# Two weight quarters per pass over the token blocks in an encoder layer's projection

## The chip, the cores and the metric

The kernel runs on one core of a Trainium2 chip. The metric is the device time of one execution in microseconds. Three runs of the kernel before took 2153.36, 2153.40 and 2154.49 us; the median is 2153.4 us.

## The reference

One layer of a hybrid encoder in float32, applied to 1024 prompt tokens and 256 sample tokens, each with 16 learned meta tokens ahead of them. A normalised input goes through one wide projection; eight heads attend globally (two key/value heads), eight in a neighbourhood window with a position bias; both results are gated by silu and go through the output projection.

```python
u = rms_norm(h, norm_w) @ w_in                     # 2048 -> 6656 columns
qa, ka, va, za, qb, kb, vb, zb = jnp.split(u, split_points(), axis=-1)
qa = apply_axial_rope(rms_norm(qa, q_norm_a), tabs)
ka = apply_axial_rope(rms_norm(ka, k_norm_a), tabs)
ya = global_gqa(qa, ka, va) * jax.nn.silu(za)
yb = neighbourhood_attention(rms_norm(qb, q_norm_b), rms_norm(kb, k_norm_b), vb, rpb) * jax.nn.silu(zb)
return h + jnp.concatenate([ya, yb], axis=-1) @ w_out
```

## The kernel before

The projection's 6656 columns are cut into 52 strips of 128 columns. A strip's weights are 16 tiles of 128 x 128 (the sum over 2048), handled as four quarters of four tiles (`WCH`). Every number is kept as a high and a low part (`wh` and `wl`, `xh` and `xl`), and each tile takes three matmuls: high by high (L227), high by low (L228), low by high (L229).

The tokens are done in two chunks. Chunk one has 512 tokens: the 256 of the sample, 240 of the prompt and the meta tokens. Chunk two has the other 784 tokens of the prompt, in two blocks of 512 and 272 columns (`BL`), each with its own bank of PSUM per strip. Their operands stay on chip as tiles `x` (512 columns) and `xb` (272 columns). The output projection follows.

`strips` (L192) projects one strip, or two or three together, over the four quarters in turn. For a quarter it loads the weights (`wr`, L206), then either casts them to `wh` on ScalarE and subtracts for `wl` on VectorE (`split`, L66 and L67), or, in chunk two, casts `wh` (L211) and loads a `wl` that chunk one stored (L210). `wh` and `wl` have four buffers each (pool `w`), so a quarter's buffers are those of the quarter four before it, and its cast and load wait until PE has read that one for the last time. Then PE goes over the blocks: in chunk two twelve matmuls of 512 columns, then twelve of 272 columns, for each quarter. After every second quarter `run_due` issues attention work that is due there.

Chunk two begins with the strips `KA` and `VA` together, in which every pass has twice the matmuls; the other 50 strips go alone. While the global heads run (`attend`), the scheduler of the framework places their matmuls among those of the projection, by its own estimate of when data is ready; later the windowed heads have fixed places (`local_heads`). The last strip is projected with `self.turn` set, with the blocks in reverse order. Transposes of V on PE are held back until the next strip has done quarter and block `self.tie`. In PE's queue, as in those of ScalarE, VectorE and SyncE, instructions stand in the order that the scheduler wrote.

Of the kernel before, what the change touches and what calls it, by code (L numbers as in the profile page):

```python
# [48 lines left out]
WCH = 4  # L49
# [10 lines left out]
class Kern:  # L60
# [131 lines left out]
    def strips(self, jobs, getx):  # L192


        nc, tc = self.nc, self.tc
        out = [[pool.tile([P, 512], F32, tag=tag, name="pp") for pool, tag in pools] for _, _, pools in jobs]
        for c in range(KT // WCH):
            ws = []
            behind = self.behind.pop(0) if self.behind else None
            for j, (s, _, _) in enumerate(jobs):  # L200
                wp = self.w if j < 2 else self.w1
                with tc.high_priority(offset=self.woff), tc.issue_after(behind) if behind else nullcontext():
                    w = self.raw.tile([P, WCH, P], F32, tag="raw", name="wr")
                    cuts = ((0, 1), (1, WCH)) if self.projected == 3 and c == 0 and not self.second else ((0, WCH),)
                    for i, e in cuts:
                        self.lastw = nc.sync.dma_start(w[:, i:e], self.io["w_in"][s][:, c * WCH + i:c * WCH + e, :]).ins  # L206
                    wh = wp.tile([P, WCH, P], F32R, tag="wh", name="wh")
                    wl = wp.tile([P, WCH, P], F32R, tag="wl", name="wl")
                    if self.second and s not in AGAIN:
                        nc.sync.dma_start(wl[:].bitcast(F32), self.wld[s][:, c * WCH:(c + 1) * WCH, :])  # L210
                        nc.scalar.copy(wh[:], w[:])  # L211
                    else:
                        for i, e in cuts:
                            self.lastsplit = self.split(wh[:, i:e], wl[:, i:e], w[:, i:e])
                            self.lasthi = self.hi
                ws.append((wh, wl))
                if not self.second and s not in AGAIN:
                    nc.sync.dma_start(self.wld[s][:, c * WCH:(c + 1) * WCH, :], wl[:].bitcast(F32))
            nb = len(jobs[0][1])
            for b in range(nb)[::-1] if self.turn else range(nb):  # L220
                for k in range(WCH):
                    kt = c * WCH + k
                    xh, xl = getx(kt)[b]
                    first, last = kt == 0, kt == KT - 1
                    for (wh, wl), ps, (_, blocks, _) in zip(ws, out, jobs):
                        p, n = ps[b], blocks[b][1]
                        nc.tensor.matmul(p[:, :n], wh[:, k, :], xh[:, :n], start=first, stop=False)  # L227
                        nc.tensor.matmul(p[:, :n], wh[:, k, :], xl[:, :n], start=False, stop=False)  # L228
                        self.lastmm = nc.tensor.matmul(p[:, :n], wl[:, k, :], xh[:, :n], start=False, stop=last).ins  # L229
                if self.turned and (c, b) == self.tie:  # L230
                    for i in self.turned:
                        tc.add_manual_dep(i, self.lastmm.name, mybir.DependencyInfo(
                            mybir.DependencyClass.NoSync, mybir.DependencyReason.DATA), reason="turned")
                    self.turned = []
            if c % 2:
                self.run_due()
        return out
# [530 lines left out]
    def chunk2(self):  # L768
# [20 lines left out]
        def k_strip(s, g, wc, rope):  # L789
            k, km = k_first(g)  # L790

            def evac(ps):
                for p, (o, n) in zip(ps, BL):
                    rp = (ct[:, o:o + n], st[:, o:o + n]) if rope else None
                    self.qk_evac(p, o, n, wc, rp, [(0, n, k[:, 0, C1P + o:C1P + o + n], k[:, 1, C1P + o:C1P + o + n])])
                return k, km
            return s, BL, evac

        def v_rows_of(s, g):

            def evac(ps):
                for p, (o, n) in zip(ps, BL):
                    self.rows_out(self.v_rows(p, o, n), n, self.vn[g], C1P + o)
            return s, BL, evac

        def v_tiles(g):

            h, l = (self.v.tile([P, 8, P], F32R, tag=f"v{i}", name="va", align_bytes=ALIGN) for i in range(2))
            nc.sync.dma_start(l[:].bitcast(F32), self.vn[g][:].rearrange("(t p) d -> p t d", p=P))
            nc.scalar.copy(h[:], l[:].bitcast(F32))  # L810
            nc.vector.tensor_tensor(out=l[:], in0=l[:].bitcast(F32), in1=h[:].bitcast(F32), op=ALU.subtract)
            return [(h[:, j, :], l[:, j, :]) for j in range(8)], self.load_vm(g)
# [12 lines left out]
        def q_strip(s, h, wc, rope):  # L825
            q = self.q.tile([P, 2, NP], F32R, tag="q", name="q", align_bytes=ALIGN)
            nc.sync.dma_start(q[:, :, :C1P].bitcast(F32), self.qd[h][:])

            def evac(ps):
                for p, (o, n) in zip(ps, BL):  # L830
                    rp = (ct[:, o:o + n], st[:, o:o + n]) if rope else None
                    self.qk_evac(p, o, n, wc, rp, [(0, n, q[:, 0, C1P + o:C1P + o + n], q[:, 1, C1P + o:C1P + o + n])])
                return q
            return s, BL, evac

        def z_strip(s, h):
            z = self.z.tile([P, NP], F32, tag="z", name="z")
            nc.sync.dma_start(z[:, :C1P], self.zd[h][:, :C1P])

            def evac(ps):  # L840
                for p, (o, n) in zip(ps, BL):
                    self.z_evac(p, o, n, [(0, n, z[:, C1P + o:C1P + o + n])])
                return z
            return s, BL, evac
# [39 lines left out]
        def run(h, q, z, k, v):  # L884
            (k, km), (v, vm) = k, v
            for b in range(4):
                c = slice(QB * b, QB * b + QB)
                keys = [(k[:, 0, o:o + P], k[:, 1, o:o + P]) for o in range(0, NP, P)]
                for _ in self.attend(q[:, :, c], z[:, c], keys, km, v, vm[:], self.yd[0][:, 2 * b:2 * b + 2, h, :]):
                    pass  # L890
# [51 lines left out]
        def fill(n):  # L942
            for _ in range(min(n, len(late))):
                pr(late.pop(0))

        for g in range(2):
            if g == 0:
                k, _ = pr(k_strip(KA, 0, kw, True), v_rows_of(VA, 0))
                self.tie = 0, 1
            else:  # L950
                k, = pr(k_strip(KA + g, g, kw, True))
                pr(v_rows_of(VA + g, g))
            v = v_tiles(g)
            for h in range(4 * g, 4 * g + 4):
                z, = pr(z_strip(ZA + h, h) + (((self.sp, "sp"),) if h == 0 else ()))
                q, = pr(q_strip(QA + h, h, qw, True))
                run(h, q, z, k, v)
                fill(FILL)
# [390 lines left out]
```

## Time and profile before

| what | us |
|---|---|
| median of three runs | 2153.4 |
| the profiled execution | 2154.02 |
| its span, first to last instruction | 2152.2 |
| PE busy | 2146.3 |
| VectorE busy | 1675.4 |
| ScalarE busy | 1204.0 |
| chunk two's projection and attention | about 599 to 1756 |

The profiled execution is the one that all rows come from. A matmul's length in the profile is longer than the distance to the next one's start, since they are pipelined: what a matmul costs the engine is read from the starts in the timeline. Idle time shows as a gap between busy stretches, and the chain of waits tells which engine the end of the program hangs on.

### The profile page before, as it was taken

The page shows a single profiled execution, that of the slowest core. Times are in us where ns is not written, and L with a number is a line of the kernel's source. Part 1 is how long each engine was busy: PE and PEld are TensorE (multiplying, and loading weights), DVE is VectorE, ACT ScalarE, POOL GpSimd, SP SyncE. Part 2 cuts the span into 40 slices and gives each one's busy share as a digit, 9 for nine tenths or more (in the row PEclk, how much of TensorE's full clock was granted, in tenths as well). Part 3 has the DMA queues.
Part 4 walks back from the last instruction along what each step waited for, and adds up shares of the span by engine and source line. Part 5 has one row for each costly group of instructions (what it writes and reads, how often), then busy time and mean ns, then how long its engine had stood idle before and what let it go on. Part 6 is the DMA issues. An engine that isn't in the chain of part 4 may idle for free.

```text
span 2152.2 us, 33487 instructions
## 1 busy us (share of the span) xinstructions
PE 2146.3 (100%) x11473; PEld 1866.0 (87%) x11473; DVE 1675.4 (78%) x3053; ACT 1204.0 (56%) x2459; POOL 530.0 (25%) x250
## 2 busy tenths in 40 slices
PE   9999999999999999999999999999999999999999
PEld 7888888888888899998998898989999888888887
DVE  7688987788874899898799898787787886545763
ACT  7677644554665777777677776444444454232230
POOL 1142422222221223232133413333333311000000
PEclk9999999999999999999999999999999999999999
DMA  8657799988654333334333334654433364762663
GB/s 294 215 186 228 242 295 319 348 280 271 212 190 133 99 100 108 109 108 125 100 105 101 106 119 128 206 162 139 133 123 124 114 214 144 241 235 89 235 226 107
DMA packets 257419, 377.21 MB, mean 175 GB/s; under 512 B 43072, under 2 KB 108768, under 8 KB 257248
## 3 DMA queue, kind: packets, MB, share of 16 engines
q1 hardware_dynamic: 257248, 375.07, 54.2%
q8 instruction: 90, 1.47, 0.3%
q14 instruction: 81, 0.66, 0.1%
HBM read 281.01 MB, written 100.38 MB: 177 GB/s over the span
## 4 chain that ended last, share of the span: by engine, by line
PE 99%; DMA 0%; DVE 0%; SPq 0%; issue 0%; ACT 0%
PE pp L227 22%; PE pp L229 22%; PE pp L228 22%; PE pq L1075 6%; PE pq L1074 6%; PE pq L1073 6%; PE po L422 3%; PE po L522 2%; PE sp L488 2%; PE sp L383 2%; PE sp L384 2%; PE sp L382 1%; PE po L423 1%; PE tp L543 0%; PE sm_ps L316 0%; PE sm_ps L315 0%
## 5 line engine op out<-in xcount | busy, mean ns | idle before, releaser
L227 PE MATMUL pp<-x,wh 128*128 128x512 f32 (+1 forms) x1664 | 654.4, 394 | 0.8 <-ACT wh L66 0.8
L228 PE MATMUL pp<-x,wh 128*128 128x512 f32 (+1 forms) x1664 | 648.3, 390 | 0.0
L229 PE MATMUL pp<-x,wl 128*128 128x512 f32 (+1 forms) x1664 | 648.2, 390 | 0.0
L229 PEld LDWEIGHTS pp<-x,wl 128*128 128x128 f32 x1664 | 312.6, 188 | 63.0 <-DVE wl L67 0.6
L227 PEld LDWEIGHTS pp<-x,wh 128*128 128x128 f32 x1664 | 312.6, 188 | 57.8 <-ACT wh L66 3.1
L228 PEld LDWEIGHTS pp<-x,wh 128*128 128x128 f32 x1664 | 312.9, 188 | 53.6
L262 POOL PARTITION_ALL_REDUCE m<-ms x78 | 237.8, 3049 | 324.5 <-ACT ms L260 251.2
L346 POOL PARTITION_ALL_REDUCE tot<-a x80 | 175.8, 2198 | 476.2 <-DVE a L343 449.2
L67 DVE TENSOR_TENSOR wl<-wr,wh 128x512 fp32r<-128x512 f32 (+2 forms) x287 | 212.6, 742 | 102.4 <-ACT wh L66 77.3
L66 ACT CAST wh<-wr 128x512 fp32r<-128x512 f32 (+2 forms) x287 | 174.0, 611 | 163.9 <-PE pp L228 148.9
L228 PE MATMUL pp<-xb,wh 128*128 128x272 f32 x832 | 240.6, 289 | 0.0
L227 PE MATMUL pp<-xb,wh 128*128 128x272 f32 x832 | 239.7, 288 | 0.0
L229 PE MATMUL pp<-xb,wl 128*128 128x272 f32 x832 | 239.4, 288 | 0.0
L1075 PE MATMUL pq<-wm,yl 128*128 128x512 f32 x560 | 218.5, 390 | 0.1
L1073 PE MATMUL pq<-wm,yh 128*128 128x512 f32 x560 | 218.5, 390 | 0.0
L1074 PE MATMUL pq<-wm,yh 128*128 128x512 f32 x560 | 218.2, 390 | 0.0
L328 POOL PARTITION_ALL_REDUCE ma<-m x80 | 109.1, 1364 | 424.7 <-DVE m L326 424.7
L228 PEld LDWEIGHTS pp<-xb,wh 128*128 128x128 f32 x832 | 156.5, 188 | 8.4
L227 PEld LDWEIGHTS pp<-xb,wh 128*128 128x128 f32 x832 | 156.6, 188 | 8.1
L229 PEld LDWEIGHTS pp<-xb,wl 128*128 128x128 f32 x832 | 157.5, 189 | 0.9
L1075 PEld LDWEIGHTS pq<-wm,yl 128*128 128x128 f32 x560 | 105.1, 188 | 22.3 <-DVE yl L67 0.5
L1073 PEld LDWEIGHTS pq<-wm,yh 128*128 128x128 f32 x560 | 105.2, 188 | 21.7
(217 smaller groups left out, 3879.3 us busy)
## 6 DMA issues: line engine op xcount, KB each, us to landing
wr<-in_w_in SPq DMA_DIRECT2D x413, 256.0 KB, 3.4
wld<-wl SPq DMA_DIRECT2D x132, 256.0 KB, 4.2
wl<-wld SPq DMA_DIRECT2D x132, 256.0 KB, 3.1
yr<-yd SPq DMA_DIRECT2D x35, 512.0 KB, 5.2
wq<-in_w_out SPq DMA_DIRECT2D x64, 256.0 KB, 5.1
td<-wq SPq DMA_DIRECT2D x64, 256.0 KB, 4.3
ww<-td SPq DMA_DIRECT2D x64, 256.0 KB, 5.4
ww<-in_w_out SPq DMA_DIRECT2D x48, 256.0 KB, 5.1
```

The lines of the kernel that those rows point to most:

```text
L66: self.hi = nc.scalar.copy(hi, full).ins
L67: return nc.vector.tensor_tensor(out=lo, in0=full, in1=hi.bitcast(F32), op=ALU.subtract).ins
L227: nc.tensor.matmul(p[:, :n], wh[:, k, :], xh[:, :n], start=first, stop=False)
L228: nc.tensor.matmul(p[:, :n], wh[:, k, :], xl[:, :n], start=False, stop=False)
L229: self.lastmm = nc.tensor.matmul(p[:, :n], wl[:, k, :], xh[:, :n], start=False, stop=last).ins
L262: nc.gpsimd.partition_all_reduce(m2[:], ms[:], P, RED.add)
L328: nc.gpsimd.partition_all_reduce(ma[:], m1[:], P, RED.max)
L346: nc.gpsimd.partition_all_reduce(tot[:], a1[:], P, RED.add)
L422: nc.tensor.matmul(po[:], vh, hl[:, i], start=j == 0, stop=False)
L1073: nc.tensor.matmul(ps, yh, wh, start=k == 0, stop=False)
L1074: nc.tensor.matmul(ps, yh, wl, start=False, stop=False)
L1075: self.lastmm = nc.tensor.matmul(ps, yl, wh, start=False, stop=k == 7).ins
```

## The change

In chunk two, for a strip that is projected alone, `strips` now collects two quarters in a list `held` before PE goes over the blocks: 24 matmuls of 512 columns over both quarters, then 24 of 272. A strip has two such rounds where it had four. Chunk one has a single block and is left as it is (`nb > 1`), as are the two strips projected together (`len(jobs) == 1`) and the last strip (`self.turn`). The tie of the V transposes is set to the first pair's block 0, which stands where quarter 0 and block 1 stood.

```diff
--- before.py
+++ after.py
@@ -194,6 +194,7 @@
 
         nc, tc = self.nc, self.tc
         out = [[pool.tile([P, 512], F32, tag=tag, name="pp") for pool, tag in pools] for _, _, pools in jobs]
+        held = []
         for c in range(KT // WCH):
             ws = []
             behind = self.behind.pop(0) if self.behind else None
@@ -217,9 +218,12 @@
                 if not self.second and s not in AGAIN:
                     nc.sync.dma_start(self.wld[s][:, c * WCH:(c + 1) * WCH, :], wl[:].bitcast(F32))
             nb = len(jobs[0][1])
+            held.append((c, ws))
+            if nb > 1 and len(jobs) == 1 and c % 2 == 0 and not self.turn:
+                continue
             for b in range(nb)[::-1] if self.turn else range(nb):
-                for k in range(WCH):
-                    kt = c * WCH + k
+                for kt, ws in [(d * WCH + k, w) for d, w in held for k in range(WCH)]:
+                    k = kt % WCH
                     xh, xl = getx(kt)[b]
                     first, last = kt == 0, kt == KT - 1
                     for (wh, wl), ps, (_, blocks, _) in zip(ws, out, jobs):
@@ -227,11 +231,12 @@
                         nc.tensor.matmul(p[:, :n], wh[:, k, :], xh[:, :n], start=first, stop=False)
                         nc.tensor.matmul(p[:, :n], wh[:, k, :], xl[:, :n], start=False, stop=False)
                         self.lastmm = nc.tensor.matmul(p[:, :n], wl[:, k, :], xh[:, :n], start=False, stop=last).ins
-                if self.turned and (c, b) == self.tie:
+                if self.turned and (held[0][0], b) == self.tie:
                     for i in self.turned:
                         tc.add_manual_dep(i, self.lastmm.name, mybir.DependencyInfo(
                             mybir.DependencyClass.NoSync, mybir.DependencyReason.DATA), reason="turned")
                     self.turned = []
+            held = []
             if c % 2:
                 self.run_due()
         return out
@@ -946,7 +951,7 @@
         for g in range(2):
             if g == 0:
                 k, _ = pr(k_strip(KA, 0, kw, True), v_rows_of(VA, 0))
-                self.tie = 0, 1
+                self.tie = 0, 0
             else:
                 k, = pr(k_strip(KA + g, g, kw, True))
                 pr(v_rows_of(VA + g, g))
```

On PE in the second half of one strip of the late fill, before. `x` and `xb` are the operands of the two blocks, `wh_18627` and `wh_18657` the high parts of quarters two and three (counted from nought), `pp_18527` and `pp_18528` the strip's two banks, and `sp` the scores of a windowed head that follow.

```order
L227 MATMUL pp_18527<-x_6793,wh_18627 128x512
...
L229 MATMUL pp_18527<-x_6817,wl_18628 128x512
L227 MATMUL pp_18528<-xb_6794,wh_18627 128x272
...
L229 MATMUL pp_18528<-xb_6818,wl_18628 128x272
L227 MATMUL pp_18527<-x_6825,wh_18657 128x512
...
L229 MATMUL pp_18527<-x_6849,wl_18658 128x512
L227 MATMUL pp_18528<-xb_6826,wh_18657 128x272
...
L229 MATMUL pp_18528<-xb_6850,wl_18658 128x272
L488 MATMUL sp_18685<-qfull_18316,kfull_18307 128x128 x2
```

The same half strip with the change:

```order
L231 MATMUL pp_18527<-x_6793,wh_18627 128x512
...
L233 MATMUL pp_18527<-x_6817,wl_18628 128x512
L231 MATMUL pp_18527<-x_6825,wh_18633 128x512
...
L233 MATMUL pp_18527<-x_6849,wl_18634 128x512
L231 MATMUL pp_18528<-xb_6794,wh_18627 128x272
...
L233 MATMUL pp_18528<-xb_6818,wl_18628 128x272
L231 MATMUL pp_18528<-xb_6826,wh_18633 128x272
...
L233 MATMUL pp_18528<-xb_6850,wl_18634 128x272
L493 MATMUL sp_18685<-qfull_18316,kfull_18307 128x128 x2
```

The 272-column matmuls of quarter two have moved behind the 512-column ones of quarter three, so that the half strip holds one step from narrow to wide less; the scores stay behind the half strip. The buffers of quarter two are read until 12 matmuls before its end.

On ScalarE, early in the global heads' work, before: `wh` is a quarter's high part, `S` and `sp` are scores, `ph` a split of probabilities, `r` and `y` belong to an attention result, `za` to a gate.

```order
L211 CAST wh_8311<-wr_8309 128x512
L66 CAST ph_7591<-S_7530 128x2x256
L66 CAST ph_7598<-S_7540 128x2x256
L353 ACTIVATE r_7606<-tot_7574 128x256
L354 ACTIVATE r_7606<-r_7606 128x256
L386 COPY S_7654<-sp_7647 128x512
L319 ACTIVATE Sl_7661<-sm_ps_7657 48x256
L304 ACTIVATE za_8229<-z_8227 128x512
L305 ACTIVATE za_8229<-za_8229 128x512
L364 COPY y_7611<-po_7576 128x256
L306 ACTIVATE za_8229<-za_8229 128x512
L211 CAST wh_8341<-wr_8339 128x512
```

The same stretch with the change:

```order
L391 COPY S_7654<-sp_7647 128x512
L324 ACTIVATE Sl_7661<-sm_ps_7657 48x256
L311 ACTIVATE za_8229<-za_8229 128x512
L359 ACTIVATE r_7606<-r_7606 128x256
L212 CAST wh_8311<-wr_8309 128x512
L212 CAST wh_8317<-wr_8315 128x512
L313 ACTIVATE za_8229<-za_8229 128x512
L369 COPY y_7611<-po_7576 128x256
L309 ACTIVATE za_8238<-z_8236 128x272
L310 ACTIVATE za_8238<-za_8238 128x272
L311 ACTIVATE za_8238<-za_8238 128x272
L391 COPY S_7738<-sp_7731 128x512
```

The casts of two following quarters had ten other instructions between them; now they stand side by side, with a gate's steps, the copy `y` of an attention result and a copy of scores behind them.

## Rows read from the trace of the kernel before

**Rows 1.** The page: span, PE busy, granted clock by slice, chain by engine.

```profile
span 2152.2 us, 33487 instructions
...
PE 2146.3 (100%) x11473; PEld 1866.0 (87%) x11473; DVE 1675.4 (78%) x3053; ACT 1204.0 (56%) x2459; POOL 530.0 (25%) x250
...
PEclk9999999999999999999999999999999999999999
...
PE 99%; DMA 0%; DVE 0%; SPq 0%; issue 0%; ACT 0%
```

**Rows 2.** Busy time by stretch: limits and length, then engines, PEclk, DMA share, GB/s.

```profile
...
599.00:1345.00 746.00, 746.00 (x4515) 669.84 (x4514) 633.31 (x1167) 534.67 (x1090) 213.03 (x99) 1.00 0.38 116
1345.00:1756.00 411.00, 411.00 (x2466) 371.24 (x2465) 320.09 (x677) 188.87 (x427) 142.07 (x76) 1.00 0.48 147
...
```

**Rows 3.** Groups by shape, PE, 599 to 1756 us: shapes xcount | busy us, mean ns.

```profile
...
L227 PE MATMUL pp<-x,wh 128*128 128x512 f32 x832 | 331.4, 399 | 0.0
L229 PE MATMUL pp<-x,wl 128*128 128x512 f32 x831 | 325.8, 392 | 0.0
L228 PE MATMUL pp<-x,wh 128*128 128x512 f32 x831 | 325.6, 392 | 0.0
L228 PE MATMUL pp<-xb,wh 128*128 128x272 f32 x832 | 240.6, 289 | 0.0
L227 PE MATMUL pp<-xb,wh 128*128 128x272 f32 x832 | 239.7, 288 | 0.0
L229 PE MATMUL pp<-xb,wl 128*128 128x272 f32 x832 | 239.4, 288 | 0.0
...
```

**Rows 4.** Timeline of PE, 1404 to 1409 us: start us, length us, instruction.

```profile
...
1404.33 0.39 PE L227 MATMUL pp<-x,wh 128*128 128x512 f32 x1
...
1405.95 0.39 PE L228 MATMUL pp<-x,wh 128*128 128x512 f32 x1
...
1407.08 0.29 PE L227 MATMUL pp<-xb,wh 128*128 128x272 f32 x1
...
1408.58 0.28 PE L519 MATMUL po<-Pm,vm 128*128 128x256 f32 x1
...
```

**Rows 5.** Timeline of PE, 620 to 637 us, around the two-strip start.

```profile
...
620.99 0.28 PE L228 MATMUL pp<-xb,wh 128*128 128x272 f32 x1
...
625.71 0.39 PE L227 MATMUL pp<-x,wh 128*128 128x512 f32 x1
...
631.15 0.29 PE L227 MATMUL pp<-xb,wh 128*128 128x272 f32 x1
...
634.14 0.40 PE L227 MATMUL pp<-x,wh 128*128 128x512 f32 x1
...
636.88 0.29 PE L227 MATMUL pp<-xb,wh 128*128 128x272 f32 x1
...
```

**Rows 6.** Timeline, VectorE and PE: a low part made, and its quarter first read.

```profile
...
635.30 0.69 DVE L67 TENSOR_TENSOR wl<-wr,wh 128x512 fp32r<-128x512 f32 x1
...
642.63 0.39 PE L227 MATMUL pp<-x,wh 128*128 128x512 f32 x1
...
```

**Rows 7.** Timeline, VectorE and PE: probabilities split, and the matmul that reads them.

```profile
...
839.20 0.68 DVE L67 TENSOR_TENSOR ph<-S,ph 128x512 fp32r<-128x512 f32 x1
...
840.24 0.39 PE L422 MATMUL po<-ph,va 128*128 128x512 f32 x1
...
```

**Rows 8.** Waits, whole kernel: who <- whom: us in total, times, longest us.

```profile
...
ACT wh L66 <- PE pp L228: 148.9, 99, 4.4
...
ACT wh L211 <- PE pp L228: 29.0, 19, 3.3
...
SPq L210 <- PE pp L229: 312.5, 100, 7.2
...
```

## The prediction

> **What bounds the kernel now.** I read four views in this order. First the page: TensorE is busy for 2146.3 of 2152.2 us, its granted clock is at the top digit in all forty slices, and the chain of work that ended last runs 99% over PE [rows 1]. Second, the busy time by stretch: chunk two, from 599 us to 1756 us, has PE busy for 746.00 of 746.00 us and for 411 of 411 us, at a granted clock of 1.00, which is the 2.4 GHz level [rows 2]. So in the stretch that the change touches no wait is left on PE. A gain can come only from instructions following each other more closely, a loss from a new wait or from a wider spacing. Third, the groups by shape: six groups of some 832 projection matmuls fill most of the stretch, three lines over 512 columns and three over 272 [rows 3]. Their durations, 392 to 399 and about 288 ns, overlap and are no cost; the cost is the distance from one start to the next, which only the timeline shows.
>
> So, fourth, the timeline. In a strip of the late fill, quarter three begins at 1404.33 right behind twelve 272-column matmuls. Its first seven 512-column matmuls take 1405.95 - 1404.33 = 1.62 us, 231 ns each; the last five take 1.13 us, 226 ns each; then twelve of 272 take 1.50 us, 125 ns each [rows 4]. Unhurried 512-column matmuls are 5.44 us for 24, so 226.7 ns each, from 625.71 to 631.15 [rows 5]. Twelve at that rate are 2.72 us, but quarter three took 2.75. **Each switch from narrow matmuls back to wide ones thus costs about 0.03 us**, spread over the seven matmuls behind it. The trace has 47 such places where twelve narrow ones stand uncut between a full wide run and the next, and each shows 30 or 31 ns. The switch from wide to narrow shows no such cost.
>
> **The change part by part.** *What it computes.* The matmuls, casts, subtractions and DMAs are the same in number and shape on every engine; chunk one and the output projection keep their order. Only chunk two's order moves, so the sum needs the differences alone.
>
> *Switches removed.* 49 strips go from four rounds over the two blocks to two. In PE's built order a 512-column projection run follows a 272-column one directly 158 times before and 70 times after: 88 fewer (49 x 2 = 98 less those that attention work cuts anyway). 88 x 0.03 = 2.6 us, all of it on the path that sets the end, because PE has no idle time there. Bounds: if every entry into a wide run is counted, from attention work too, there are about 305 before and 235 after; 70 at the 0.02 us that one switch after 24 narrow ones cost (2.74 us for twelve from 634.14, against 2.72) make 1.4 us [rows 5]. At the other end the remaining switches could get cheaper too: the wide run at 625.71 follows 38 narrow matmuls (from 620.99) and runs at 226.7 ns from its first one on [rows 5]. If all 70 that remain lost their 0.03 as well, 88 + 70 = 158 of them make 4.7 us. I take 2.6, since the 47 uncut places are nearest to what is removed.
>
> *The narrow runs themselves.* 24 in a row take 634.14 - 631.15 = 2.99 us, 124.6 ns each, as the twelve do (125) [rows 4, 5]. Longer runs neither gain nor lose: 0.
>
> *Weight buffers held longer.* A half strip lasts 24 x 0.2267 + 24 x 0.1246 = 8.43 us. Before, a quarter's buffer came free 4.2 us after its first matmul and was wanted again four quarters later, 12.7 us on. Now a pair's first quarter comes free after 24 x 0.2267 + 12 x 0.1246 = 6.9 us and its buffer is wanted 16.9 us after the pair's start: 9.9 us to refill, 2.8 less. The second comes free at 8.4 and is wanted at 19.6: 11.1 us, 1.6 less. What covers that: the tightest quarter that the change touches has its subtraction done at 635.30 + 0.69 = 635.99 and is first read at 642.63, 6.6 us later [rows 6]. 6.6 - 2.8 leaves 3.8, so the price is 0. Without that cover a late quarter would cost PE what is missing, at most once per half strip.
>
> *What waits for these buffers.* The casts on ScalarE wait for PE's release (148.9 us in 99 waits over the kernel in L66, 29.0 us in L211), and SyncE's loads of the stored low parts do the same (312.5 us in 100 waits) [rows 8]. Behind a waiting cast on ScalarE stand evacuations and softmax steps; behind a waiting load on SyncE stand stores of y and z and the next loads. The built order now sets casts in twos, near the release, with an evacuation of attention and a copy of scores right behind one such pair. Cost 0 as long as attention's results keep their lead on PE; the thinnest lead is a subtraction that ends at 839.20 + 0.68 = 839.88 for a matmul that starts at 840.24: 0.36 us [rows 7]. It is the least of 128 such groups; 11 have under 1 us and the median is 2.8. This is the term with the widest bounds, and the slower rival below.
>
> *Transposes of V.* They are tied behind the first pass of block 0, now 24 x 0.2267 = 5.4 us into the next strip where it was 4.2. The store and the loads behind it start 1.2 us later, with whole strips of 17 us before the values are read: 0; if that cover were gone, 1.2 us for each of ten strips. *Evacuation.* Block 0 of a strip is finished 3.0 us ahead of its end where it was 1.5, and each bank is wanted no sooner: 0, and no gain either, because PE waits for no bank now.
>
> *Sum.* -2.6 us. The profiled execution took 2154.0 us (span 2152.2); it would take 2151.4. The median of the runs is 2153.4, 0.6 below that execution, so I forecast **2150.8 us**, 0.12% less.
>
> **The rivals.** *No gain: the extra is a debt of the narrow matmuls.* 240 columns at 2.4 GHz are 100 ns, so from 226.7 one would expect 126.7 for a narrow matmul; 124.6 is 2.1 less, 25 ns over twelve, about what the wide ones behind then pay back. If PE only repays there what it ran ahead, then 24 narrow ones leave twice the debt and merging saves nothing: 2153.4 us, within a few tenths. Against it: the wide run after 24 narrow ones paid 0.02 and the one after 38 paid nothing [rows 5]. But those are one place each, both near two strips projected together. The Trainium skill (TensorE: Matmul & The Clock Gate, "Wait — 56ns, not 53.3ns?") has its own form of this: each warm matmul takes its columns over 2.4 GHz plus a fixed 2.5 ns, whatever stands before it. By that rule a 512-column matmul would take 215.8 ns and the order would be worth nothing, the same 2153.4; the trace shows 226.7 at rest and 231 behind a switch, so the rule does not hold here as it stands.
>
> *Slower: casts at the head of ScalarE's queue.* A cast that waits up to 2.8 us longer for its buffer pushes the exponentials and splits behind it. The 11 value groups that lead PE by under 1 us (about 0.75 in the mean) would each make PE wait up to 2.8 - 0.75 = 2 us. The rival decides from the second such group on for any loss, and from the fourth for a loss over 0.2% (4.3 + 2.6 = 6.9 us). Six of them give 12 - 2.6 = 9.4 more: 2162.8 us. Against it: attention keeps its place among the strips in PE's built order to within half a strip, and the median lead of 2.8 us just swallows the delay.
>
> *More than forecast.* The remaining switches lose their cost too, as at 625.71: 2153.4 - 4.7 = 2148.7 us. That the change does not do what it says is told from the built order: 88 of 98 rounds are gone.
>
> **How the numbers follow.** Forecast, a gain of 1.4 to about 4: 0.58. More than forecast: 0.10. Debt, no gain: 0.18. Slower: 0.14, of which 0.03 stays within 4.3 us. About 0.2%, 4.3 us, is what a measurement of this kernel tells from no change: faster by more 0.10, within 0.79, slower by more 0.11. The range leaves out the end of the largest gain and most of the slower rival: 2148.9 to 2155.5.
>
> **What would show it.** In the changed kernel's timeline of the late fill, wide runs of 24 should have about seven matmuls at 231 ns and then seventeen at 226 to 227; if about fourteen are at 231, the debt is right. PE should stay busy for the whole of chunk two; a gap ahead of a value matmul of the lines that are L422 and L423 now, released by VectorE or ScalarE, means the slower rival, and one ahead of a projection matmul released by a cast means that the buffers' cover was misjudged. The stretches before 599 us and after chunk two should keep their lengths; if not, the sum has left something out.

## The result: 2163.4 us, 0.45% slower

The kernel after takes 2163.42 us (median of 5 runs, 2162.46 to 2165.01) against 2154.04 us (5 runs), a ratio of 1.0045 [1.0034, 1.0056]: 9.4 us more, outside the range of 2148.9 to 2155.5. Its profiled execution took 2162.46 us with a span of 2160.7, 8.5 us above the span of [rows 1].

The page of the kernel after:

```profile
span 2160.7 us, 33474 instructions
...
PE 2146.8 (99%) x11473; PEld 1864.7 (86%) x11473; DVE 1679.3 (78%) x3053; ACT 1198.7 (55%) x2459; POOL 532.7 (25%) x250
...
PEclk9999999999999999999999999999999999999999
...
PE 18%; DVE 2%; issue 1%; DMA 0%; ACT 0%; POOL 0%; SPq 0%; DVEq 0%; POOLq 0%; ACTq 0%
```

PE is busy as long as before and the clock is as high; the span grew by waits. The chain of work that ended last, which ran 99% over PE [rows 1], can now be followed back over some 21% of the span only: PE's 18% are nearly all the output projection, and around its start the chain leaves PE for VectorE, ScalarE and DMA.

What PE waited for in the kernel after (who <- whom: us in total, times, longest us):

```profile
PE sp L387 <- ACT S L391: 2.2, 1, 2.2
PE po L524 <- DVE Pm L343: 1.9, 1, 1.9
PE tp L548 <- DVE vt L294: 1.6, 1, 1.6
PE warm L649 <- DVE wz L646: 1.2, 1, 1.2
PE pp L231 <- ACT wh L66: 1.2, 3, 0.6
PE pq L1080 <- DVE yl L67: 0.9, 1, 0.9
PE sp L321 <- DVE q L67: 0.5, 1, 0.5
PE po L427 <- DVE ph L67: 0.5, 2, 0.3
```

The kernel before has two such rows, the warm-up's 1.2 and 0.8 for the first casts. The rest, 2.2 + 1.9 + 1.6 + 0.4 + 0.9 + 0.5 + 0.5 = 8.0 us, is new. Each wait costs PE some 0.17 us more than the gap that the profile gives, since the length of the matmul before it runs on over its distance (at 838.05 the gap is 2.16 and the starts lie 2.33 us too far apart); the longer span is what is left of these waits when the saving of the switches is taken off. But for 0.4 behind the first casts, ahead of 9 us, they lie in or right behind chunk two, and there none is released by a cast or a load of the projection's weights: they are single steps of attention or evacuation, a score copy, `Pm`, the V rows `vt`, q, `ph`, and a piece of y.

Line numbers of after stand up to 5 higher than before's (6 or 7 in some variants). What [rows 8] showed of before, the waits for PE's release of a weight buffer, is in the kernel after 109.6 + 13.9 instead of 148.9 + 29.0 us for casts, and 267.8 instead of 312.5 for SyncE's loads: less in total, though the buffers are held longer; the longest single waits grew, from 4.4 to 6.7 and from 7.2 to 10.2 us.

```profile
ACT wh L66 <- PE pp L232: 109.6, 79, 6.7
...
ACT wh L212 <- PE pp L232: 13.9, 16, 2.9
```

```profile
SPq L211 <- PE pp L233: 267.8, 86, 10.2
```

The longest wait, in the timelines of PE, VectorE, ScalarE and GpSimd of the kernel after (start us, length us, instruction [idle before <- releaser]):

```profile
834.59 2.48 DVE L282 TENSOR_TENSOR rs_r<-t,rs_r 128x272 f32<-128x272 f32 x1
...
837.10 0.42 ACT L66 CAST q<-rs_r 128x272 fp32r<-128x272 f32 x1 [2.85 <-DVE rs_r L282]
837.42 0.58 ACT L391 COPY S<-sp 128x512 f32<-128x512 f32 x1
...
834.49 3.27 POOL L267 PARTITION_ALL_REDUCE m<-ms  x1
...
838.05 0.39 PE L387 MATMUL sp<-q,kf 128*128 128x256 f32 x1 [2.16 <-ACT S L391]
```

PE wants a score bank back. The copy that frees it stands in ScalarE's queue behind a cast of q, which waits for a VectorE step that took 2.48 us, beside an all-reduce on GpSimd.

### The profile page after: what moved, and what is told of

Read it like the earlier page. It is cut to its first block, busy times and chain, and to the rows that moved or that the text cites. A ratio compares the mean times of both kernels' runs of the same rounds, so it can differ in the third digit from the quotient of the medians.

```text
span 2160.7 us, 33474 instructions
## 1 busy us (share of the span) xinstructions
PE 2146.8 (99%) x11473; PEld 1864.7 (86%) x11473; DVE 1679.3 (78%) x3053; ACT 1198.7 (55%) x2459; POOL 532.7 (25%) x250
## 5 line engine op out<-in xcount | busy, mean ns | idle before, releaser
L233 PEld LDWEIGHTS pp<-x,wl 128*128 128x128 f32 x1664 | 312.5, 188 | 61.6 <-DVE wl L67 0.3
L267 POOL PARTITION_ALL_REDUCE m<-ms x78 | 231.5, 2968 | 342.5 <-ACT ms L265 281.1
L66 ACT CAST wh<-wr 128x512 fp32r<-128x512 f32 (+2 forms) x287 | 172.9, 610 | 126.9 <-PE pp L232 109.6
L333 POOL PARTITION_ALL_REDUCE ma<-m x80 | 116.9, 1461 | 439.8 <-DVE m L331 417.4
```

The source lines that it names most:

```text
L66: self.hi = nc.scalar.copy(hi, full).ins
L267: nc.gpsimd.partition_all_reduce(m2[:], ms[:], P, RED.add)
L333: nc.gpsimd.partition_all_reduce(ma[:], m1[:], P, RED.max)
```

## The experiments

Two theories stood at first. **Held buffers**: a pair's weights are held longer, so casts on ScalarE and loads on SyncE wait at the head of their queues, with softmax steps behind them. **Places**: the scheduler ordered everything anew, and single results now stand too late for PE. Later runs ask which of the change's parts brings them in. The table gives what each kernel lost, as the start of the same matmul less its start in the kernel before, from the two traces.

| kernel | median us | of before | ratio, 95% | lost at 1389 us | at 1678 us | at 1757 us | at the end |
|---|---|---|---|---|---|---|---|
| after | 2163.4 | 2154.0 | 1.0045 [1.0034, 1.0056] | 4.5 | 3.6 | 7.3 | 8.4 |
| keep_pe | 2180.3 | 2153.6 | 1.0124 [1.0109, 1.0139] | 26.0 | 24.8 | 25.7 | 25.6 |
| hold_pe | 2179.9 | 2153.6 | 1.0122 [1.0107, 1.0137] | 25.8 | 24.4 | 25.3 | 24.8 |
| back | 2154.8 | 2153.7 | 1.0005 [0.9996, 1.0014] | 2.0 | 1.3 | 1.2 | 0.7 |
| back_act | 2160.2 | 2153.7 | 1.0029 [1.0017, 1.0041] | 9.9 | 9.1 | 8.9 | 8.8 |
| tie | 2155.1 | 2153.6 | 1.0006 [0.9996, 1.0016] | 1.8 | 1.8 | 1.8 | 1.3 |
| tie10 | 2157.8 | 2153.9 | 1.0018 [1.0009, 1.0028] | 4.0 | 4.1 | 4.1 | 3.6 |
| hold | 2158.5 | 2153.9 | 1.0022 [1.0013, 1.0031] | 2.6 | 1.9 | 1.8 | 3.5 |
| atie01 | 2159.5 | 2153.9 | 1.0026 [1.0017, 1.0036] | 0.9 | 0.0 | 3.8 | 5.2 |
| atie20 | 2162.3 | 2153.9 | 1.0041 [1.0026, 1.0056] | 5.2 | 4.3 | 9.0 | 9.1 |
| noend | 2160.5 | 2153.9 | 1.0031 [1.0020, 1.0041] | 5.0 | 4.2 | 5.0 | 6.1 |
| noend01 | 2155.5 | 2153.8 | 1.0006 [0.9997, 1.0015] | 1.8 | 0.9 | 1.2 | 1.9 |

The columns are a strip early in the late fill, the start of the last head's strips, the start of the output projection, and the end of the span. Rows of one batch share their runs of the kernel before.

**Order alone: two that isolated nothing.** The first runs wrote one kernel's order of ScalarE, VectorE, GpSimd and SyncE into the other.

```diff
+            k.tc.add_manual_dep(by_name[b], a, mybir.DependencyInfo(
+                mybir.DependencyClass.NoSync, mybir.DependencyReason.DATA), reason="keep order")
```

This runs over a table of instruction names for each engine and ties each to the one ahead of it; from keep_pe on the table has PE too.

Expected of keep_all:

> The changed kernel, but ScalarE, VectorE, GpSimd and SyncE keep, instruction for instruction, the order that they had in the kernel before; only PE's order has the merged rounds (78 direct steps from 272 to 512 columns, 158 before, 70 in the change). Order theory (the loss comes from the order in which VectorE and ScalarE were re-planned): 80 steps x 0.03 us saved and no PE wait over 0.3 us in chunk two, so 2154.0 - 2.4 = 2151.6 us. Held-buffer theory (the loss comes from weight buffers that PE frees later, with casts and loads waiting at the head of their queues): the buffers are freed as late as in the change, so 2158 to 2165 us, with the same kind of PE waits.

Expected of swap:

> The kernel before, with PE's rounds by quarters as they were, but the other four engines in the order of the changed kernel. Order theory: the loss comes along with the order, about 2154 + 9 to 12 less what the shifted leads give back, so 2159 to 2166 us. Held-buffer theory: the buffers come free as early as before, so 2154 us, within 1.5.

2173.6 us (1.0091 [1.0076, 1.0106]) and 2185.1 us (1.0148 [1.0133, 1.0163]): both theories missed both. PE's order was left to the scheduler, and it had moved attention on PE up to 9.7 us later among the projection matmuls in keep_all, up to 14.4 us in swap (counted at 0.2267 and 0.1246 us per matmul). So neither run tells what one change of order costs by itself; the next runs write out PE's order too.

**Holding alone, order kept.** keep_pe is the changed kernel's rounds; hold_pe has the rounds before, but the last narrow step of quarter A runs behind quarter B's wide run, so that A's buffer comes free at 6.9 us instead of 4.2. All five engines keep the order before, but for 49 attention matmuls in each that stand 2.3 to 5.4 us later on PE. All of these run after 1650 us, when by the table the loss was already there.

```diff
+                if pair and b == 1 and c % 2 == 0:
+                    tail = todo.pop()
+                elif pair and b == 1:
+                    todo.insert(0, tail)
```

Expected of keep_pe:

> The changed kernel's rounds (two quarters at a time) with every engine's order written out: attention stands on PE at the same count of projection matmuls as in the kernel before, and ScalarE, VectorE, GpSimd and SyncE keep the order before but for a few dozen rows. Place theory (the changed kernel loses because the re-planned order queues single results of VectorE and ScalarE too late for PE): the saving of 2.6 us stays and the 8.4 us of waits go, 2151.3 us (2150 to 2153). Held-buffer theory (holding a pair's weights longer delays the casts and all that stands behind them): the holding is all still there, 2157 to 2163 us, with waits of PE behind results that stand behind casts.

Expected of hold_pe:

> The kernel before with its four rounds, all engines' order kept; only the last three 272-column matmuls of the first quarter of each pair are run behind the second quarter's 512-column run, so that the first quarter's weight buffer is held until 6.9 us after its start instead of 4.2, as in the changed kernel. Held-buffer theory: 2158 to 2163 us. Place theory: 2154 us (2153.4 to 2155), as the kernel before, since the number of switches from narrow to wide matmuls stays.

2180.3 and 2179.9 us. The place theory falls for this order: with nothing merged, the longer holding alone costs 26 us, and the two traces lose it at the same places. The held-buffer theory had the direction, but its 2157 to 2163 us were 17 us short. ScalarE's waits for PE in hold_pe:

```profile
ACT wh L66 <- PE pp L234: 151.2, 88, 7.3
ACT wh L211 <- PE pp L234: 126.4, 61, 6.5
```

L211 casts waited 29.0 us in 19 waits before [rows 8]; now it is 126.4 in 61. One of them in the timelines of ScalarE, VectorE and PE of hold_pe:

```profile
1236.74 0.62 ACT L211 CAST wh<-wr 128x512 fp32r<-128x512 f32 x1 [4.64 <-PE pp L234]
1237.26 1.13 ACT L66 CAST ph<-S 128x512 fp32r<-128x512 f32 x2
...
1237.91 1.29 DVE L67 TENSOR_TENSOR ph<-S,ph 128x512 fp32r<-128x512 f32 x2 [3.69 <-ACT ph L66]
...
1238.65 0.50 PE L428 MATMUL po<-ph,va 128*128 128x512 f32 x1 [1.58 <-DVE ph L67]
```

The cast stands idle for 4.64 us until PE gives the buffer back, the probabilities' casts stand behind it, VectorE waits 3.69 for them and PE 1.58. The weight itself is in no hurry. PE's wait is put down to `ph`, and no view names the weight cast as its cause: it is found one step up, in ScalarE's queue.

**The waiting instructions put back.** back is keep_pe, with the buffers held just as long; casts, loads and subtractions that would wait for the later release stand behind what their engine did in that time before (and the late 49 matmuls, behind 1650 us, are back at their places). back_act does so with casts and subtractions, on ScalarE and VectorE, alone. One of 89 such places on ScalarE, from keep_pe to back:

```diff
-L212 CAST wh<-wr 128x512
 L324 ACTIVATE Sl<-sm_ps 48x256
 L550 COPY vl<-tp 128x512
 L391 COPY S<-sp 128x512
-L408 ACTIVATE S<-S 128x512 x2
+L408 ACTIVATE S<-S 128x512
+L212 CAST wh<-wr 128x512
+L408 ACTIVATE S<-S 128x512
```

Expected of back:

> The changed kernel's rounds with attention at the places on PE that it has in the kernel before, as in keep_pe, and the order before on the other engines but for one rule: where a cast, a load of stored low parts or a subtraction has to wait for a weight buffer that is now held up to 2.7 us longer, it is put behind what its engine did in that time in the kernel before (89 casts, 141 loads on SyncE, 25 subtractions get a later place). The buffers are held just as long as in keep_pe. If the 26.7 us of keep_pe come from casts that wait at the head of ScalarE's queue with softmax steps behind them: these waits go and the saving of the switches shows, 2151 us (2150 to 2155). If they come from the buffers being held at all, or from weights that arrive late: 2170 to 2180 us.

Expected of back_act:

> As back, but only ScalarE's casts (and VectorE's subtractions behind them) are put back; SyncE keeps the order before, with its loads of stored low parts waiting at the head of its queue. If ScalarE's queue alone makes the loss: 2154 to 2157 us. If SyncE's waiting loads, with the next weight loads behind them, make a good part: 2160 us or more.

2154.8 us: of the 26.7 us, 25.6 are gone, though the saving of the switches does not show, for the time is level with the kernel before. So in this order the loss lies neither in the holding as such nor in late weights, but in what stands behind the instruction that waits. Putting back ScalarE's casts, with VectorE's subtractions, gives 2180.3 - 2160.2 = 20 us; SyncE's loads give the other 5.3, of which this, in back_act on SyncE and PE, is the largest piece:

```profile
1248.54 0.33 SPq L211 DMA_DIRECT2D wl<-wld  x1
1248.91 0.54 SPq L832 DMA_DIRECT2D q<-qd  x1
...
1253.04 0.36 PE L387 MATMUL sp<-q,kf 128*128 128x256 f32 x1 [2.46 <-DMA q<-qd]
```

The load of low parts is issued only when PE has given its buffer back, and the load of q behind it is 2.5 us late for PE. With the slower clock that followed (last section) the piece is 2.5 + 1.7 = 4.2 us.

Expected of back2:

> As back, but in the global heads the waiting casts and loads are put 1.5 us behind the release of their buffer instead of 0.1, and at 845 us on VectorE two sums of the softmax stand behind a subtraction that PE waits for. In back, PE's waits in chunk two came to some 2.3 us, 1.3 of them behind casts that still waited (1198.0 and 871.3) and 0.5 at 845. Cast theory: these 1.8 us go, 2153.0 us (2152 to 2154). If a weight now came late, a wait of PE behind a cast or a subtraction wl would show, and 2155 us or more.

2156.6 us (1.0013 [1.0005, 1.0022]), so this missed. The casts came later still, but the wait at 1199 us, behind GpSimd, stayed, and 0.8 us at 853 was new. Part of what PE still waits for does not hang on the casts; which part was not followed up.

**The changed kernel's own order.** The scheduler does not keep the order: in the kernel after it plans the casts elsewhere, and they wait less in total. Is what is left a few late places?

```diff
+L391 COPY S<-sp 128x512
 L66 CAST q<-rs_r 128x272
-L391 COPY S<-sp 128x512
...
+L343 TENSOR_TENSOR Pm<-Sm,Pm 16x256
 L67 TENSOR_TENSOR wl<-wr,wh 128x512
...
-L343 TENSOR_TENSOR Pm<-Sm,Pm 16x256
...
+L294 TENSOR_TENSOR vt<-pp,rb_320 128x272
 L67 TENSOR_TENSOR wm<-ww,wm 128x512 x4
-L294 TENSOR_TENSOR vt<-pp,rb_320 128x272
```

Expected of patch:

> The changed kernel with its whole order kept, but for six instructions on ScalarE and VectorE that are moved ahead of one to eight others: the score copy for which PE waits at 835.5, the softmax steps behind Pm at 1741, vt at 1757.6 and yl at 1764. Place theory: these waits are 2.3 + 2.0 + 1.7 + 1.1 = 7.1 us and go, 2156.3 us (2155.5 to 2158). Held-buffer theory: the cause is elsewhere and the time comes back at the next weights, 2162 to 2164 us.

2162.4 us (1.0039 [1.0024, 1.0054]). The two named waits at 835 and 1741 lost their releasers, but the time came back within 15 us: at 842 to 850 PE waits four times for the next softmax results, 2.2 us in all; at 1741 it waits for a bank that `y` L364 frees, at 1758 for a copy `vl`. The supply behind PE is late there as a whole, not at one step. Held buffers foretold the number; nothing in this run shows that they are the reason.

**New plans, with and without holding.** tie and tie10 change one number in the kernel before, the tie of the V transposes; hold is hold_pe with the scheduler left free; atie01 and atie20 are the changed kernel with another tie.

```diff
-                self.tie = 0, 1
+                self.tie = 0, 0
```

That is tie; tie10 has (1, 0). In the changed kernel, which has (0, 0), atie01 sets (0, 1) and atie20 (2, 0).

Expected of tie:

> The kernel before with one number changed: the transposes of V in the global heads are tied behind the strip's first pass, (0, 0), and not behind its second, (0, 1). No rounds are merged and no buffer is held longer; the scheduler orders the work anew. Place theory: about 2.0 us of new waits on PE before the late fill, between 1200 and 1400 us, released by VectorE: 2155.9 us (2154.8 to 2158). Held-buffer theory: no change, 2153.4 to 2154.3 us.

Expected of tie10:

> The kernel before with the global heads' tie at (1, 0), behind the second quarter's first pass: a new plan without merged rounds and without longer holding. If any new plan costs some 8 us by itself: 2160 us or more. If the holding is needed for that: 2153.5 to 2156.5 us, as tie.

Expected of hold:

> As hold_pe (the kernel before, but the first quarter of each pair gives its weight buffer back at 6.9 us instead of 4.2), now with the scheduler free to order the work anew. If what is left in the changed kernel (8.4 us) is what the longer holding costs after the scheduler has planned for it: 2158 to 2164 us. If it is the accident of that one plan: like the other plans without holding (tie: 2155), 2153.5 to 2156.5 us.

Expected of atie01:

> The changed kernel with the tie of the kernel before, (0, 1): another plan with the same rounds and the same holding. If the holding makes the loss: 2159 to 2167 us. If the loss is the accident of one plan, the times of such plans scatter, and one near 2152 to 2156 us is as likely.

Expected of atie20:

> The changed kernel with the tie at (2, 0), behind the second pair's first pass: a third plan with the same rounds and the same holding. Expected as for atie01: 2159 to 2167 us if the holding makes the loss, anything from 2152 us on if it is the accident of the plan.

Plans without holding or merging cost 1.5 us (tie, not told from none, though where the place theory put it) and 3.9 us (tie10, between its two ranges). hold, at 4.6, atie01 and atie20 all came out where the held-buffer theory put them. But hold is not told from tie10, which holds nothing: that holding by itself costs more than planning anew does, once the scheduler plans for it, is not shown, nor that it costs nothing. Merged plans scatter from 2159.5 to 2163.4. By the table, atie01 has lost nothing by the start of the last head, and 5.2 us behind it.

**Where the rounds are merged.** noend leaves the last head's K, Q and V strips by quarters, with the change's tie; noend01 with the tie before; late and late2 merge in the late fill alone, late with the change's tie, late2 with the tie before in the global heads.

```diff
-            if nb > 1 and len(jobs) == 1 and c % 2 == 0 and not self.turn:
+            if nb > 1 and len(jobs) == 1 and c % 2 == 0 and not self.turn and self.merge:
...
+                self.merge = len(late) > 4
```

The last line stands in `fill`; late and late2 also switch `self.merge` off in the global heads, and late2 from the last but one head on.

Expected of noend:

> The changed kernel, but the last head's strips K, Q and V are also done by quarters. Order theory: the waits at 1741 us (2.0) and 1757.6 us (1.7) and the 1.1 us ahead of the output projection were made where the last strips' work crowds VectorE, so some 4.9 us go: 2158.5 us, if the rest of the order stays. Held-buffer theory: three of 49 strips are a sixteenth of a loss of 12 us: 2162.6 us.

Expected of noend01:

> The plan of atie01, with the last head's K, Q and V strips by quarters as in noend. In atie01's trace the start of the last head's strips stands 0.1 us earlier than in the kernel before, and the 5.3 us of loss all come behind it. If merging in the last head makes that loss: these 5.3 us go but for the 1 us at the start of the output projection that noend kept, 2154 us (2153 to 2155). If they come whatever the rounds are there: 2158 us or more.

Expected of late:

> Merged rounds only in the strips that are filled in while the windowed heads run, not in those of the global heads and not in the last head's. Order theory: the fixed places of the windowed heads leave their leads alone, 17 strips x 2 x 0.031 us are saved: 2153.0 us, no PE wait over 0.3 us. Held-buffer theory: a third of the held rounds make a third of the loss: 2156 to 2158 us.

Expected of late2:

> Merged rounds in the late fill alone (the V strips of the last heads, with little attention among them), the tie of before kept in the global heads: 26 switches fewer. Cast theory: little stands behind the casts there, so 26 x 0.03 = 0.8 us less and no new wait, 2152.8 us (2152.2 to 2154). Theory that any new plan costs some us: 2155 us or more.

Taking the last head out gives 3.0 us from after to noend and 4.1 us from atie01 to noend01. The tie alone, with the same rounds, gives 5.0 us: 2160.45 for noend, 2155.45 for noend01. Together these are 8.0 of the 9.4 us, and noend01, with the rounds still merged in 46 of the 49 strips, loses 1.7. Of the two expectations noend came out half way between its two numbers, and noend01 half a microsecond above its range. PE's waits in noend01 where atie01 had 1.9 for `Pm`, 1.1 for `vt` and 1.1 for `yl`:

```profile
PE pp L231 <- ACT wh L66: 1.2, 3, 0.7
PE warm L649 <- DVE wz L646: 1.2, 1, 1.2
PE pq L1081 <- DVE yl L67: 0.8, 1, 0.8
PE sp L321 <- DVE q L67: 0.6, 1, 0.6
PE po L427 <- DVE ph L67: 0.2, 1, 0.2
```

late came to 2156.4 us (1.0013 [1.0004, 1.0023]) and late2 to 2154.0 us (1.000 [0.999, 1.001]). late has the number of the held-buffer theory, but not for its reason: its trace has lost 2.0 us at 1389 us, early in the late fill, as tie has (1.8), which merges nothing, and no more than 1.2 at 1678, behind its merged rounds. late2 has gained 0.5 at both places. No version beat the kernel before: the best with merged rounds, late2, back and noend01, are level with it.

## Why the prediction was wrong

**Switches: the saving is there, but smaller, and a switch has no one price.** In the timeline of PE in the kernel after, 24 wide matmuls behind 24 narrow ones:

```profile
659.86 0.40 PE L231 MATMUL pp<-x,wh 128*128 128x512 f32 x1
...
661.47 0.39 PE L232 MATMUL pp<-x,wh 128*128 128x512 f32 x1
...
665.32 0.29 PE L231 MATMUL pp<-xb,wh 128*128 128x272 f32 x1
```

The first seven take 1.61 us, 230 ns each, the other seventeen 3.85, 226.5 each: 0.02 us for this switch, where one behind twelve narrow ones cost 0.03. The rival of the debt, which wanted fourteen slow ones, falls with that. But the number of narrow ones ahead does count. In hold_pe nine of them stand between two wide runs, and the wide run behind them is unhurried from its first matmul:

```profile
1449.27 0.29 PE L233 MATMUL pp<-xb,wh 128*128 128x272 f32 x1
...
1450.40 0.39 PE L233 MATMUL pp<-x,wh 128*128 128x512 f32 x1
...
1451.99 0.39 PE L234 MATMUL pp<-x,wh 128*128 128x512 f32 x1
...
1453.12 0.29 PE L233 MATMUL pp<-xb,wh 128*128 128x272 f32 x1
```

Seven matmuls take 1.59 us here, 227 ns each, and all twelve 2.72; 37 of the 43 such places in that trace show no extra at all. So "each switch costs 0.03" was a reading of twelve narrow ones, and what makes the price stays open. In the late fill the kernel after gains 0.06 us a strip on the kernel before, two switches of 0.03, as forecast. But the term of 2.6 us is about 2. Summed over every wide run in back, as distances less 226.7 ns: in the late fill 39 entries from narrow matmuls cost 1.2 us before and 6 cost 0.2 after; in the global heads 118 entries cost 2.6 us and 63 cost 1.4, so 2.2 us are saved. Entries from attention went from 105 to 123 and from 1.7 to 2.1 us, or from 2.7 to 2.8 with the few above 0.06 us counted in. That leaves 1.8 to 2.1 us, between the bound of 1.4, which had counted such entries, and the 2.6 that I took. I took a switch at 0.03 throughout; the 118 cost 0.022.

**Weight buffers: the cover was taken at the wrong place.** I set the 2.8 us of later release against the 6.6 us that a subtraction lies ahead of PE [rows 6], and that held: no wait of PE in chunk two, in the kernel after, is released by one of these weights. But the release is awaited by an instruction at the head of a queue, and there the cover is that of whatever stands behind it. hold_pe prices this: 26 us with the order kept. I had written down this mechanism, with its price worked from eleven thin leads, as a rival at 0.14, and argued against it with the median lead of 2.8 us. The median is no cover: a queue passes the delay of every cast on. That this rival's 2162.8 us lie 0.6 us from the measured 2163.4 is luck. It had six value matmuls wait 2 us each; in the kernel after two of them wait 0.5 us in all, and the casts wait less than before.

**What failed: "Cost 0 as long as attention's results keep their lead on PE" [rows 7].** They did not keep it. I took the leads of the kernel before as if its order stood still; the scheduler's order is new from 600 us on, and each new plan brings its own leads. I had also measured the leads of one kind of result only, the split probabilities `ph`: they are 0.5 of the 8.0 us of new waits, and 7.1 are a freed score bank, `Pm`, `vt`, y and q, whose leads I had not looked at. With eleven of 128 leads under 1 us and the thinnest 0.36, a plan that happens to wait nowhere is not the rule: tie10 loses 3.9 us with nothing changed but a tie.

**The tie: priced 0, cost 3.9 and 5.0 us in merged rounds** (after against atie01, noend against noend01), 1.5 alone, not told from none. The transposes were early enough, as I had it; that the tie also decides the plan I left out.

**The last head: not priced at all.** Every merged plan of the scheduler's loses about 5 us between 1678 us and the end (after 4.8, atie01 5.2, atie20 4.8, of which 1.7 is the clock behind a wait of 3.0 us for `vt`; by quarters -0.5 to 1.9). It need not be so: back, merged there too, gains 0.6. What the plan does there, in the timelines of ScalarE, VectorE and PE of the kernel after:

```profile
1756.18 0.62 ACT L66 CAST wm<-ww 128x512 fp32r<-128x512 f32 x1 [0.60 <-DMA ww<-in_w_out]
...
1756.83 2.15 DVE L67 TENSOR_TENSOR wm<-ww,wm 128x512 fp32r<-128x512 f32 x3 [0.52 <-ACT wm L66]
1758.89 0.43 DVE L294 TENSOR_TENSOR vt<-pp,rb 128x272 f32<-128x272 f32 x1
...
1759.47 0.52 PE L548 MATMUL tp<-ident,vt 128*128 128x128 f32 x3 [1.58 <-DVE vt L294]
```

`vt` stands behind subtractions of output weights, which wait for casts, and these for a DMA. In the kernel before, four such subtractions stood ahead of it and none of them waited.

What stays open: whether the scatter of the plans (2159.5 to 2163.4 merged, 2155.1 and 2157.8 not) is larger for merged rounds in the global heads, or whether the change's tie merely drew badly. Three merged plans and two others do not tell. More weight buffers, which would take the holding away, were not tried.

## What to carry to other kernels

When a buffer is released later, ask not when its next content is needed but which instruction waits for the release, in which queue, and what stands behind it; the wait then shows under another name. In a kernel whose bounding engine never waits, a new order can only keep that or lose it: price any edit that makes the scheduler plan anew with the spread of such plans, got from a neutral edit, here 1.5 to 3.9 us, before a gain of 2.6. And try such a change without the end of its stretch: there it met the next stage's loads, and 3 to 4 of the 9.4 us came from there.

## What the runs showed of the hardware

**VectorE beside GpSimd.** Additions and products of 128x272 in chunk two of the kernel before take 433 ns in the mean and at most 447 in 104 cases clear of an all-reduce on GpSimd; in the kernel after, 46 that overlap one take 549 in the mean and up to 2476 ns, as at 834.59 above. But the stretch is the exception: 38 of the 46 take 443 ns or less, and in the kernel before 29 that overlap one take 442 in the mean, with one of 844. Steps of 48x256 that read one input from the accumulator banks do not stretch (at most 418 ns in 18 cases); nor do four of that shape with both inputs in on-chip memory (at most 410 ns). So a new plan also decides which result an all-reduce holds up. The Trainium skill (SBUF — State Buffer, "SBUF: two separate sides") says that a VectorE instruction with two inputs in that memory and a GpSimd instruction that reads it exclude each other, the first holding the ports to its end. The few long steps may be that (the one at 834.59 ends 0.7 us before the all-reduce beside it); the many that overlap one and do not stretch do not show it.

**The clock behind a wait.** In back_act PE waited from 1250.5 to 1253.0 us. Busy time by stretch (limits and length, engines, granted clock, DMA share, GB/s):

```profile
1250.00:1253.00 3.00, 0.58 (x5) 0.35 (x3) 2.97 (x7) 1.30 (x4) 1.52 (x1) 1.00 0.83 228
1253.00:1255.00 2.00, 1.96 (x13) 1.99 (x14) 2.00 (x6) 1.87 (x5) 0.00 (x0) 0.78 0.01 2
1255.00:1257.00 2.00, 2.00 (x7) 1.65 (x6) 2.00 (x5) 2.00 (x5) 0.00 (x0) 0.50 0.11 37
1257.00:1259.00 2.00, 2.00 (x9) 1.62 (x8) 2.00 (x5) 2.00 (x6) 0.00 (x0) 0.87 0.76 210
```

The granted clock was 0.78, 0.50 and 0.87 behind it, 0.50 being the 1.2 GHz level, and wide matmuls started 0.43 us apart. At 2 x (0.22 + 0.50 + 0.13) = 1.7 us this wait cost two thirds more than its length. Waits of 2.4 us in keep_pe and hold_pe and of 3.0 us in atie20 were followed by the same 1.7 us. The wait of 2.16 us in the kernel after, up to 838.05, left the clock at 1.00.
